# Sparse attention beside an RWKV recurrence: scores and weighted sums per head of 64 channels instead of in the 128-channel latent space

## The chip, the cores and the metric

The kernel runs on one core of one Trainium2 chip. The metric is the device time of one execution in microseconds (us), lower is better. The core's engines are named as in the profile: PE is TensorE, with PEld for its weight loads, DVE is VectorE, ACT is ScalarE, POOL is GpSimd, and SP is SyncE, which here only issues DMAs.

## The reference, cut to what is computed

One layer on a sequence of 2048 tokens of width 1024. A projection of the normalised input feeds two branches of 512 channels each, and an output projection adds their result to the input. The first branch is an RWKV recurrence in 8 heads of 64 channels. The second is attention in 8 heads of 64 channels, in which each query uses at most 256 keys, chosen by separate index heads; keys and values of all heads come from one latent vector of 128 channels per token.

```python
y_rwkv = rwkv7_branch(p_shift, g_rwkv, ...)
c_q, c_kv = rmsnorm(q_down, q_norm_g), rmsnorm(kv_down, kv_norm_g)      # 256 and 128 channels
q = (c_q @ w_uq).reshape(B, T, ATTN_HEADS, HEAD_DIM)
q_abs = jnp.einsum('bthd,hrd->bthr', q, w_uk) * (HEAD_DIM ** -0.5)      # query in the latent space
...
_, idx = lax.top_k(score, topk)                                         # the chosen keys
c_sel = jax.vmap(lambda c, i: c[i])(c_kv, idx)
s = jnp.einsum('bqhr,bqkr->bhqk', qa, c_sel)
p = jax.nn.softmax(s, axis=-1)
o_lat = jnp.einsum('bhqk,bqkr->bqhr', p, c_sel)
...
o = jnp.einsum('bthr,hrd->bthd', o_lat, w_uv)
y = jnp.concatenate([y_rwkv, o * silu(gate)], axis=-1) @ w_out
out = rmsnorm(x + y, final_g)
```

## The kernel before

The program has four parts, which a scheduler interleaves when the kernel is built; the order of the instructions on each engine is fixed from then on, and an engine whose next instruction waits does nothing else meanwhile.

**SA** (`phase_as`) projects the input, for four groups of 512 tokens, in blocks of 128 columns. Its matmuls are in fp32r, a single-pass form of lower precision, so each operand is split into a high and a low part and a product takes three passes (`proj`, L574 to L576). `visit` runs rounds of such blocks with small jobs between them; the index heads and the choice of keys (`picker`) write one mask per block of 128 queries. `latent` (L702) normalises the latent vector c_kv and stores it twice, channels first (`d_ckT`) and tokens first (`d_ck`), each as a high and a low part; the normalised query vector goes to `d_cq`.

**T** (`phase_t`) is the attention. An item is 256 queries of a pair of heads. `onto` brings the queries into the latent space (12 matmuls of 256 columns, L1171 to L1173). For each block of 128 queries and each head, scores come in chunks of up to 512 keys, in three passes (L1197 to L1199); DVE adds the mask and takes the maximum (L1201), ACT exponentiates each chunk (L1208). The weights are transposed on PE (L1217), copied by ACT as a high part (L1220), and DVE makes the low part (L1221). The weighted sums run for both heads together as 256 columns in three passes (L1225, L1226, L1229). At the end of an item the row sums are spread (L1238, L1241), and six matmuls of 256 columns lead out of the latent space (L1248 to L1250). The masks are loaded once, since the items go through the four pairs of heads for the same queries.

**R** (`phase_r`) is the recurrence, in 16 chunks of 128 tokens that depend on each other. `prepare(n)` loads and scales a chunk and makes its systems E (`prep`, L910, L912; issued with low priority through `later`); `inverse` inverts their 32x32 diagonal blocks on POOL: DMAs write E to DRAM (`du`, L950) and bring it back with a system on each partition (`A`, L952), 31 pairs of POOL instructions follow (L961, L963), and DMAs carry the result back (`dx` L964, `TT` L968). `prep2` makes what else the chain needs (L920 to L940). `chain` then takes the state through the two halves of the chunk: products with the state (L981, L988), `solve` (L997) with the inverses, L1015, `solve` again, the new state (L1022). `tail` normalises the result (L1032 to L1044; the power on POOL is in the helper `rpow`, L127) and writes it to `d_y` for two units in turn through one buffer `yo` (L1050 to L1054). In the program text `prepare(n + 1)` stands ahead of `chain(n)`.

**W** (`phase_w`) is the output projection: for each of 16 blocks of 128 tokens it loads `yl` from `d_y` (L1296), splits it, and runs 48 matmuls of 512 columns (L1306 to L1309); the result is added to the input, normalised and stored (L1310 to L1316). Its tiles lie where those of T lay, so W begins after T's end.

T and R share PE and the other engines. All DMAs of R and W and most of T's go through the one queue of SP in a fixed order; T's latents and queries go through POOL's.

Of the kernel before, what the change touches and what calls it, by code (L numbers as in the profile page):

```python
# [36 lines left out]
def kernel(ctx: ExitStack, tc: tile.TileContext, x, norm_g, w_in, mu_shift, w0, w_up, a0, a_up,  # L37
# [19 lines left out]
    # ------------------------------------------------------------------ scratch in DRAM  # L57
# [5 lines left out]
    d_ckT = [dram([128, T], F32, f"d_ckT{i}") for i in range(2)]  # L63
    d_ck = [dram([128, NB, 128], F32, f"d_ck{i}") for i in range(2)]
# [9 lines left out]
    # ------------------------------------------------------------------ constants  # L74
# [4 lines left out]
    ones2 = const([128, 2], F32, "ones2")          # columns: ones on rows 0-63, ones on rows 64-127  # L79
# [3 lines left out]
    bad = const([128, NB], F32, "bad")             # rows whose choice of keys is to be made again  # L83
# [49 lines left out]
    def later(n=1):  # L133
        """what is issued inside gives way to what is issued outside, and inside with less"""
# [50 lines left out]
def picker(e, tls, KI, wi_a, wi_s, fast, spare=None):  # L185
    """choice of keys"""
    tc, dma, V, S, G, PE, f32, nm = e.tc, e.dma, e.V, e.S, e.G, e.PE, e.f32, e.nm
    wqh = tls([128, 2, 4, 2, 64], F32R, "wqh")   # query projection of the index heads, each head twice
    wql = tls([128, 2, 4, 2, 64], F32R, "wql")
    cmask = tls([128, 128], F32, "cmask")        # -LOW where key <= query, else LOW  # L190

    def setup_s():
# [10 lines left out]
        # blocks 0 and 1 keep every key that is not after the query  # L203
# [7 lines left out]
    def queries(j):  # L211
        """q_idx^T of blocks 2j, 2j+1: [128 (twice the 64 channels), head, 256]; high and low parts"""
# [55 lines left out]
    def quick(b, xs, on_act):  # L268
        """the same from the scores in float16: bisection in the cube root of the threshold, then the exact
        threshold among the (at most eight) scores left; marks the rows where more than those were left"""  # L270
# [15 lines left out]
        # each column of vm holds a score, so at least 256 scores reach their minimum  # L286
# [15 lines left out]
        # cube roots of the ends (negated for the scalar engine's counts), and the halves of their distance  # L302
# [22 lines left out]
        # the eight largest of the rest, and the one wanted  # L325
# [9 lines left out]
        G.tensor_tensor(col(48), col(28), col(31), op=OP.subtract)       # how many of the equal scores stay  # L335
# [10 lines left out]
    def exact(b, xs, on_act):  # L346
        """largest threshold that at least TOPK scores reach, found bit by bit in an order-preserving
        integer form of the scores; then the additive mask, ties going to the lowest index"""
# [18 lines left out]
        def search(data, cnt0, cand, thr, res):  # L367
            """16 steps of bisection; cnt0: first of 16 columns for the counts; thr: TOPK or a column"""
# [17 lines left out]
        def rejected(cnt0, thr, res):  # L386
            """the largest count below the threshold"""
# [6 lines left out]
        # columns: 0-15, 16-31 counts; 32, 33 candidates; 34 top, 35 low; 36 counted above; 37 k2; 38 its form  # L394
# [53 lines left out]
def again(env):  # L448
    """the choice of keys by the general search, the attention and the output once more"""
# [23 lines left out]
def phase_as(env):  # L473
    """projections in, and the choice of keys"""
# [33 lines left out]
    # lora weights [decay | a]: high parts on rows 0-63, low parts on rows 64-127;  # L508
    # of each, rows 0-31 take the decay's inputs and rows 32-63 those of a
# [11 lines left out]
    def load_w(cols, pad=False, raw=None):  # L521
        """columns of w_in as high and low parts [128, 8, 128]; cols: (target, source, width)"""
# [56 lines left out]
    def shift(pm, blk, mu, om):  # L579
        """token shift of the psum block"""  # L580
# [37 lines left out]

    def split_store(t, dst, sl):
        """fp32 tile -> high and low parts -> dram"""  # L620
        h = t2(F32R)
        l = t2(F32R)
        S.activation(h, t, AF.Copy)
        V.tensor_tensor(l, t, f32(h), op=OP.subtract)
        dma(dst[0][sl], f32(h))
        dma(dst[1][sl], f32(l))

# [10 lines left out]
    def index_group(g, t, qr):  # L638
        """index keys and weights, and the queries' latent"""
# [34 lines left out]
        pb = row_spread(rsq, 1)  # L674
# [403 lines left out]
def phase_t(env):  # L1078
# [52 lines left out]
    for u in (uvh, uvl):  # L1131
        V.memset(f32(u)[:, :, 1], 0.0)
# [212 lines left out]
```

## Time and profile before

| | |
|---|---|
| median of 3 runs | 2168.61 us (2166.92 to 2169.61) |
| span of the profiled execution | 2172.8 us; its time is not listed apart from the span |
| PE busy | 1926.4 us, 89% of the span, 13094 instructions |
| DVE, ACT, POOL busy | 1457.3, 1095.8, 872.3 us |
| SA alone on PE | 0 to 895 us |
| T and R on PE | 895 to 1955 us; T's last instruction falls in chunk 15 of R's 16 |
| rest of R, and W | 1955 to 2172.8 us |

The span is that of one profiled execution, the times are those of runs of their own; the span is 4.2 us above their median. The page's busy times are sums over the whole span, so they are read by stage; the matmuls overlap in the pipeline, so the cost of one is taken from the distance of two starts rather than from its duration. In the chain of waits, a piece is followed back from the last instruction to what released it.

### The profile page before, as it was taken

The page shows a single profiled execution, that of the slowest core. Times are in us where ns is not written, and L with a number is a line of the kernel's source. Part 1 is how long each engine was busy: PE and PEld are TensorE (multiplying, and loading weights), DVE is VectorE, ACT ScalarE, POOL GpSimd, SP SyncE. Part 2 cuts the span into 40 slices and gives each one's busy share as a digit, 9 for nine tenths or more (in the row PEclk, how much of TensorE's full clock was granted, in tenths as well). Part 3 has the DMA queues.
Part 4 walks back from the last instruction along what each step waited for, and adds up shares of the span by engine and source line. Part 5 has one row for each costly group of instructions (what it writes and reads, how often), then busy time and mean ns, then how long its engine had stood idle before and what let it go on. Part 6 is the DMA issues. An engine that isn't in the chain of part 4 may idle for free. (4 is left out here: it accounts for less than half of the span.)

```text
span 2172.8 us, 37051 instructions
## 1 busy us (share of the span) xinstructions
PE 1926.4 (89%) x13094; PEld 1606.2 (74%) x13094; DVE 1457.3 (67%) x3331; ACT 1095.8 (50%) x2328; POOL 872.3 (40%) x2114
## 2 busy tenths in 40 slices
PE   5999988979788889788989889898898998887997
PEld 4787776757676677577878778787787887776886
DVE  5554597896969798676767766677566776554332
ACT  4345845345375444345555656565555565454221
POOL 1112325444344656445543454345444345442110
PEclk9899998989999999789999999999899999998999
DMA  7442432226243222633332223212222112116343
GB/s 240 154 128 59 128 128 68 92 68 241 65 142 118 74 73 68 197 80 81 80 80 52 58 61 92 58 39 76 62 59 73 53 33 63 47 33 201 122 148 108
DMA packets 255891, 206.69 MB, mean 95 GB/s; under 512 B 75088, under 2 KB 219856, under 8 KB 254544
## 3 DMA queue, kind: packets, MB, share of 16 engines
q1 hardware_dynamic: 244656, 183.78, 28.6%
q0 software_dynamic: 11040, 20.45, 3.2%
q8 instruction: 105, 1.72, 0.3%
q14 instruction: 90, 0.74, 0.1%
HBM read 127.31 MB, written 76.87 MB: 94 GB/s over the span
## 5 line engine op out<-in xcount | busy, mean ns | idle before, releaser
L574 PE MATMUL pm<-xh,wh 128*128 128x512 f32 x800 | 330.2, 415 | 20.7 <-DVE t L585 12.7
L575 PE MATMUL pm<-xl,wh 128*128 128x512 f32 x800 | 327.6, 410 | 0.0
L576 PE MATMUL pm<-xh,wl 128*128 128x512 f32 x800 | 326.6, 409 | 0.0
L1208 ACT ACTIVATE sc<-sc,mx 128x512 f32<-128x512 f32 (+3 forms) x320 | 206.9, 650 | 68.9 <-DVE mx L1206 68.4
L1201 DVE CUSTOM_DVE_ANT_0 sc<-s,mk 128x512 f32<-128x512 f32 (+3 forms) x320 | 188.5, 605 | 60.3 <-PE tr L1217 33.5
L1221 DVE TENSOR_TENSOR ptl<-tr,pth 128x512 fp32r<-128x512 f32 (+1 forms) x288 | 186.0, 654 | 52.0 <-ACT pth L1220 48.7
L1220 ACT ACTIVATE pth<-tr 128x512 fp32r<-128x512 f32 (+1 forms) x288 | 160.9, 570 | 116.6 <-PE tr L1217 95.2
L961 POOL TENSOR_TENSOR Xtmp<-Xr,A 128x60 f32<-128x60 f32 (+24 forms) x496 | 148.6, 300 | 165.6 <-DMA A<-du 131.5
L574 PEld LDWEIGHTS pm<-xh,wh 128*128 128x128 f32 x800 | 158.4, 199 | 61.6 <-DVE t L585 15.9
L1217 PE MATMUL tr<-ident,sc 128*128 128x128 f32 x1088 | 177.8, 282 | 18.0 <-DVE ptl L1221 12.6
L576 PEld LDWEIGHTS pm<-xh,wl 128*128 128x128 f32 x800 | 157.2, 196 | 35.8
L575 PEld LDWEIGHTS pm<-xl,wh 128*128 128x128 f32 x800 | 157.7, 197 | 35.1
L963 POOL TENSOR_TENSOR Xr<-Xr,Xtmp 128x60 f32<-128x60 f32 (+24 forms) x496 | 150.2, 303 | 34.6
L1225 PE MATMUL om<-pth,ck 128*128 128x256 f32 x544 | 159.0, 312 | 0.8 <-DVE ga L1251 0.8
L1197 PE MATMUL s<-ckT,qh 128*128 128x512 f32 (+2 forms) x320 | 135.7, 424 | 26.7 <-DVE mx L1201 26.1
L1217 PEld LDWEIGHTS tr<-ident,sc 128*128 128x128 f32 x1088 | 131.4, 145 | 25.2 <-DVE ptl L1221 13.0
L314 ACT ACTIVATE mk<-x,st 128x1920 bf16<-128x1920 f16 (+5 forms) x72 | 98.0, 1361 | 100.1 <-POOL st L311 100.1
L1226 PE MATMUL om<-pth,ck 128*128 128x256 f32 x544 | 146.5, 289 | 0.0
L246 ACT ACTIVATE rl<-lg,wi 128x512 f32<-128x512 f32 (+3 forms) x152 | 93.0, 628 | 94.3 <-DVE xs L251 41.0
L1229 PE MATMUL om<-ptl,ck 128*128 128x256 f32 x544 | 127.7, 311 | 14.4 <-DVE ptl L1221 14.4
L317 DVE TENSOR_SCALAR_CACHE_REDUCE mk<-x,st 128x2048 bf16<-128x2048 f16 (+5 forms) x72 | 120.7, 1676 | 1.5
L1199 PE MATMUL s<-ckT,ql 128*128 128x512 f32 (+2 forms) x320 | 118.4, 380 | 3.4 <-DVE ql L1175 3.4
(345 smaller groups left out, 4790.7 us busy)
## 6 DMA issues: line engine op xcount, KB each, us to landing
wraw<-in_w_in_dram SPq DMA_DIRECT2D x42, 512.0 KB
d_rw<-t SPq DMA_DIRECT2D x80, 256.0 KB
ld<-d_rw SPq DMA_DIRECT2D x32, 640.0 KB
A<-du SPq DMA_DIRECT2D x16, 512.0 KB
yl<-d_y SPq DMA_DIRECT2D x16, 512.0 KB
xr<-in_x_dram SPq DMA_DIRECT2D x16, 512.0 KB
out_dram<-xr SPq DMA_DIRECT2D x16, 512.0 KB
cq<-d_cq POOLq DMA_DIRECT2D x30, 256.0 KB, 3.8
```

The costliest lines, as they stand in the source:

```text
L574: PE.matmul(pm, wh[:, k], XH[g][:, k], start=k == 0, stop=False)
L575: PE.matmul(pm, wh[:, k], XL[g][:, k], start=False, stop=False)
L576: PE.matmul(pm, wl[:, k], XH[g][:, k], start=False, stop=k == KD - 1)
L961: G.tensor_tensor(tmp[:, :m, :w], Xr[:, :m, s:s + 1].to_broadcast([128, m, w]), A[:, s:s + 1, s + 1:].to_broadcast([128, m, w]), op=OP.mult)
L963: G.tensor_tensor(Xr[:, :m, s + 1:], Xr[:, :m, s + 1:], tmp[:, :m, :w], op=OP.add)
L1201: V.tensor_tensor_reduce(out=sc[:, :w], in0=pS[:, :w], in1=mks[qb][:, c0:c0 + w], scale=1.0, scalar=LOW, op0=OP.add, op1=OP.max, accum_out ...
L1208: S.activation(sc[:, :w], sc[:, :w], AF.Exp, bias=mx[:, 4:5], accum_out=sums4[:, q, h, i:i + 1])
L1217: PE.transpose(pt[:, i, h], PR[h][(kb + i) // 4][0][:, (kb + i) % 4 * 128:(kb + i) % 4 * 128 + 128], ident)
L1220: S.activation(th[:, :m], pt[:, :m], AF.Copy)
L1221: V.tensor_tensor(tw[:, :m], pt[:, :m], f32(th)[:, :m], op=OP.subtract)
L1225: PE.matmul(pof, ck[0][:, kb + i], rh, start=kb + i == 0, stop=False)
L1226: PE.matmul(pof, ck[1][:, kb + i], rh, start=False, stop=False)
```

## The change

The attention works per head. SA now projects onto the heads: `query_weights` and a query job of 96 matmuls of 512 columns make q for 64 channels per head (`d_q`, high and low parts); behind `latent`, `keys_of` and `values_of` (48 matmuls of 512 columns each) make keys (`d_kt`, high and low) and values (`d_vt`, tokens first) of the heads, which replaces 16 transposes and the storing of `d_ckT` and `d_ck`. In T a unit is 128 queries of a pair of heads, and the units go through all 16 blocks for one pair and then for the next, so each mask is loaded four times. The 128 rows of a key tile hold the 64 channels of a head as a high part and below it as a low part, and the query tile holds its high (or low) part twice; two passes then give the scores. One exponential runs over the whole row of a head. The transposed weights stay in fp32, without a low part, and the weighted sums are fp32 matmuls of 128 columns onto 64 output rows, one head in each half of the array. All of T's loads are now on SP's queue: 64 masks, 256 query pieces, 64 key pieces, 16 value tiles, 64 gates, and 64 stores. Per execution T has 2944 PE instructions, and had 4380. R and W are unchanged, with line numbers 60 and 4 higher.

```diff
+        def keys_of(p):
+            def job():
+                h, l = parts
+                pk = pst([128, 512], "tr", 2)
+                ws = slice(p * 128, p * 128 + 128)
+                PE.matmul(pk, wh[:, 0, ws], h, start=True, stop=False)
+                PE.matmul(pk, wh[:, 0, ws], l, start=False, stop=False)
+                PE.matmul(pk, wl[:, 0, ws], h, start=False, stop=True)
+                split_store(pk, e.d_kt, (slice(None), p, slice(g * 512, g * 512 + 512)))
+            return job
...
+        rows = [tl([128, T], F32, "sc", 4) for h in range(2)]
...
+            for h in range(2):
+                pS = pst([128, C], "s", 2)
+                PE.matmul(pS[:, :wp], qh[:, h, qs], k[:, h, :wp], start=True, stop=False)
+                PE.matmul(pS[:, :wp], ql[:, h, qs], k[:, h, :wp], start=False, stop=True)
...
+            S.activation(rows[h][:, :n], rows[h][:, :n], AF.Exp, bias=mx[:, h, 4:5], accum_out=sums[:, h:h + 1])
...
-                    PE.matmul(pof, ck[0][:, kb + i], rh, start=kb + i == 0, stop=False)
-                    PE.matmul(pof, ck[1][:, kb + i], rh, start=False, stop=False)
...
-                    PE.matmul(pof, ck[0][:, kb + i], rl, start=False, stop=kb + i == qb)
...
+        def values(kb, m, w):
+            for i in range(m):
+                v = VT[p, (kb + i) // 4]
+                for h in range(2):
+                    PE.matmul(po[HALF[h]], v[:, (kb + i) % 4, HALF[h]], w[:, i, h],
+                              start=kb + i == 0, stop=kb + i == b)
...
+    units = [(p, b) for p in range(NP) for b in range(NB)]
```

In the order rows below, a row is one instruction or a run of equal ones: line, operation, output and inputs, shape, and how many. First PE inside T, before: `tr` are the transposes, `s` the scores, `om` the weighted sums.

```order
L1229 MATMUL om_20461<-ptl_20483,ck_2111_13334 128x256 x2
L1225 MATMUL om_20461<-pth_20497,ck_2111_13334 128x256
L1226 MATMUL om_20461<-pth_20497,ck_2112_13335 128x256
L1225 MATMUL om_20461<-pth_20497,ck_2111_13334 128x256
L1226 MATMUL om_20461<-pth_20497,ck_2112_13335 128x256
L1217 MATMUL tr_20507<-ident,sc_20410 128x128
L1217 MATMUL tr_20507<-ident,sc_20441 128x128
L1217 MATMUL tr_20507<-ident,sc_20410 128x128
L1217 MATMUL tr_20507<-ident,sc_20441 128x128
L1197 MATMUL s_20664<-ckT_2109_13332,qh_20197 128x512
L1198 MATMUL s_20664<-ckT_2110_13333,qh_20197 128x512
L1199 MATMUL s_20664<-ckT_2109_13332,ql_20198 128x512
```

And PE inside T with the change:

```order
L1237 MATMUL tr_19196<-ident,sc_19041 128x128
L1237 MATMUL tr_19196<-ident,sc_19042 128x128
L1237 MATMUL tr_19196<-ident,sc_19041 128x128
L1237 MATMUL tr_19196<-ident,sc_19042 128x128
L1237 MATMUL tr_19203<-ident,sc_19041 128x128
L1237 MATMUL tr_19203<-ident,sc_19042 128x128
L1237 MATMUL tr_19203<-ident,sc_19041 128x128
L1237 MATMUL tr_19203<-ident,sc_19042 128x128
L1203 MATMUL s_19192<-kt_19088,q_3596_19031 128x256
L1204 MATMUL s_19192<-kt_19088,q_3597_19036 128x256
L1246 MATMUL om_19173<-pt_19179,vt_18452 64x128 x4
L1246 MATMUL om_19173<-pt_19186,vt_18452 64x128 x3
```

The three passes of 256 columns over `pth` and `ptl` have become runs of mostly four fp32 matmuls of 128 columns on 64 output rows, alternately in the two halves of the array; T has 273 such runs, and they stand between transposes and scores, which use the whole array.

Second, PE in a late chunk of R, from the middle of `chain`: before, with T's work (`s`, `om`, `tr`) beside it.

```order
L1015 MATMUL ch_11921<-SV_11437,E_11298 32x64
L1015 MATMUL ch_11921<-SV_11457,E_11334 32x64
L1197 MATMUL s_20645<-ckT_2109_13332,qh_20197 128x384
L1198 MATMUL s_20645<-ckT_2110_13333,qh_20197 128x384
L1199 MATMUL s_20645<-ckT_2109_13332,ql_20198 128x384
L1229 MATMUL om_20461<-ptl_20468,ck_2111_13334 128x256 x2
L1217 MATMUL tr_20492<-ident,sc_20410 128x128
L1217 MATMUL tr_20492<-ident,sc_20441 128x128
L1217 MATMUL tr_20492<-ident,sc_20410 128x128
L1217 MATMUL tr_20492<-ident,sc_20441 128x128
```

The same place with the change, in a chunk after T's end, where `po` is W's:

```order
L1075 MATMUL ch_12281<-SV_11890,E_11767 32x64
L990 MATMUL rp_12267<-ident,BK_12132 128x128 x4
L1057 MATMUL ch_12281<-R_12280,TT_11860 32x64 x8
L1310 MATMUL po_20848<-wh_20136,yh_20840 128x512
L1311 MATMUL po_20848<-wl_20137,yh_20840 128x512
L1310 MATMUL po_20848<-wh_20136,yh_20840 128x512
L1311 MATMUL po_20848<-wl_20137,yh_20840 128x512
L1310 MATMUL po_20848<-wh_20136,yh_20840 128x512
L1311 MATMUL po_20848<-wl_20137,yh_20840 128x512
L1310 MATMUL po_20848<-wh_20136,yh_20840 128x512
```

T's last instruction now falls at the end of R's chunk 8; in chunks 9 to 16 only W stands beside the chain. Ahead of the second solve of chunks 9 to 16 stand 242, 432, 480, 528, 576, 624, 672 and 720 of W's 768 matmuls, so from chunk 11 on one block of 48 falls in each chunk, in four pieces inside the chain: behind the first half's second solve, behind its new state, and on both sides of the second half's reads. It is the block whose `yl` comes from the chunk just ended.

Third, SP's queue around the loads of the inverse: before.

```order
L950 DMA du_10975<-E_10924 32x8x32 x2
L950 DMA du_10975<-E_10960 32x8x32 x2
L1054 DMA d_y<-yo_10886 128x2x128
L952 DMA A_10977<-du_10975 128x1x1024
L1048 DMA gr_10895<-d_gr 128x2x128
L874 DMA ld_11313<-d_rw 128x10x128
L878 DMA vt_11278<-d_v 128x2x192
L1054 DMA d_y<-yo_10894 128x2x128
L1048 DMA gr_11261<-d_gr 128x2x128
```

With the change, in a late chunk:

```order
L1010 DMA du_12156<-E_12105 32x8x32 x2
L1114 DMA d_y<-yo_12067 128x2x128
L1010 DMA du_12156<-E_12141 32x8x32 x2
L1108 DMA gr_12076<-d_gr 128x2x128
L934 DMA ld_12494<-d_rw 128x10x128
L1012 DMA A_12158<-du_12156 128x1x1024
L1114 DMA d_y<-yo_12075 128x2x128
L1108 DMA gr_12442<-d_gr 128x2x128
L938 DMA vt_12459<-d_v 128x2x192
L1300 DMA yl_20841<-d_y 128x8x128
```

The `A` of chunk n + 2 stood behind the two `du` and the first `d_y<-yo` of chunk n, and now a 640 KB `ld` stands ahead of it too; the second `d_y<-yo` stays behind `A`, and W's `yl` for chunk n is now behind that store at once.

## Rows read from the trace of the kernel before

**Rows 1.** Busy time by stage: start:end, length, PE, PEld, DVE, ACT, POOL, PEclk, DMA share, GB/s

```profile
0.00:895.00 895.00, 776.08 (x3448) 620.23 (x3448) 670.51 (x1235) 437.68 (x678) 352.56 (x684) 0.93 0.36 115
895.00:1955.00 1060.00, 955.52 (x8528) 827.80 (x8529) 705.03 (x1998) 596.39 (x1528) 488.39 (x1349) 0.93 0.27 68
1955.00:2172.80 217.80, 194.80 (x1120) 158.13 (x1119) 81.77 (x99) 61.77 (x123) 31.34 (x83) 0.95 0.45 145
```

**Rows 2.** Groups of instructions: count, then busy us and mean ns, then idle before

```profile
L1225 PE MATMUL om<-pth,ck 128*128 128x256 f32 x544 | 159.0, 312 | 0.8 <-DVE ga L1251 0.8
...
L1199 PE MATMUL s<-ckT,ql 128*128 128x512 f32 (+2 forms) x320 | 118.4, 380 | 3.4 <-DVE ql L1175 3.4
...
L1171 PE MATMUL om<-cq,wch 128*128 128x256 f32 x128 | 38.5, 303 | 0.7 <-DVE mx L1206 0.7
```

**Rows 3.** PE's timeline in W: start us, duration, instruction

```profile
2073.53 0.39 PE L1306 MATMUL po<-wh,yh 128*128 128x512 f32 x1
...
2077.15 1.98 PE L1309 MATMUL po<-wh,yl 128*128 128x512 f32 x8
```

**Rows 4.** PE's timeline in a chain: an x8 here is 4 fp32 matmuls

```profile
1424.03 0.66 PE L981 MATMUL ch<-S,X 128*64 128x128 f32 x8
1424.52 0.63 PE L988 MATMUL ch<-SV,E 128*64 128x64 f32 x16
```

**Rows 5.** The chain of waits, T and R on PE: start us, length, piece

```profile
1289.50 0.59 PE rp L981 x8
...
1290.55 0.32 PE om L1229
1290.87 0.12 PE om L1225
...
1293.29 0.44 PE rp L981 x8
...
1297.23 0.44 PE tr L1217 x4
```

**Rows 6.** SP's timeline: issues of A; first two and last of 16

```profile
941.93 0.83 SPq L952 DMA_DIRECT2D A<-du  x1
...
985.97 0.56 SPq L952 DMA_DIRECT2D A<-du  x1
...
1930.31 0.56 SPq L952 DMA_DIRECT2D A<-du  x1
```

**Rows 7.** POOL's timeline: first and last step of the last chunk's inverse

```profile
1940.26 0.24 POOL L961 TENSOR_TENSOR Xtmp<-Xr,A 128x31 f32<-128x31 f32 x1 [10.19 <-DMA A<-du]
...
1963.58 0.22 POOL L963 TENSOR_TENSOR Xr<-Xr,Xtmp 128x8 f32<-128x8 f32 x1
```

**Rows 8.** The chain of waits: a store issued right behind A

```profile
1930.98 9.49 DMA d_y<-yo
```

**Rows 9.** ACT's timeline at R's end: idle before and releaser in brackets

```profile
2046.32 0.39 ACT L1026 ACTIVATE y<-rp 128x256 f32<-128x256 f32 x1
...
2063.74 0.81 ACT L1050 ACTIVATE yo<-ch,gnb,gng 128x128 f32<-128x128 f32 x2 [3.60 <-DMA d_y<-yo]
...
2077.61 1.06 ACT L1297 ACTIVATE yh<-yl 128x1024 fp32r<-128x1024 f32 x1 [2.44 <-DMA yl<-d_y]
```

**Rows 10.** DVE's timeline, the same stretch

```profile
2052.11 0.68 DVE L1041 TENSOR_TENSOR y<-y,gst 128x512 f32<-128x512 f32 x1
```

**Rows 11.** SP's timeline, the same stretch

```profile
2061.80 0.37 SPq L1054 DMA_DIRECT2D d_y<-yo  x1
...
2073.72 0.52 SPq L1296 DMA_DIRECT2D yl<-d_y  x1
```

**Rows 12.** Two windows of 10 us at T's beginning, columns as in rows 1

```profile
950.00:960.00 10.00, 5.06 (x45) 4.24 (x42) 3.15 (x14) 2.42 (x7) 5.10 (x18) 0.79 0.34 95
960.00:970.00 10.00, 9.27 (x40) 8.29 (x39) 6.50 (x19) 3.96 (x11) 7.12 (x21) 0.52 0.08 20
```

**Rows 13.** The chain of waits behind the last matmul

```profile
2160.77 0.70 DVE xr L1310
```

More of the change, by code (lines that the diff above doesn't have):

```diff
@@ L674, in index_group @@
         pb = row_spread(rsq, 1)
+        ch = tls([128, 2, 512], F32R, "qh")
+        cl = tls([128, 2, 512], F32R, "ql")
         for j in range(2):
             V.scalar_tensor_tensor(qr[j], qr[j], e.qgc[:, j:j + 1], pb, op0=OP.mult, op1=OP.mult)
-            split_store(qr[j], e.d_cq, (slice(None), j, slice(g * 512, g * 512 + 512)))
+            split(qr[j], ch[:, j], cl[:, j])
+        dma(e.d_cq[0][:, :, sl], f32(ch))
+        dma(e.d_cq[1][:, :, sl], f32(cl))
+        for p in range(NP):
+            pq = pst([128, 512], "pm", 3)
+            cs = slice(p * 128, p * 128 + 128)
+            for j in range(2):
+                PE.matmul(pq, uq[0][:, j, cs], ch[:, j], start=j == 0, stop=False)
+                PE.matmul(pq, uq[0][:, j, cs], cl[:, j], start=False, stop=False)
+                PE.matmul(pq, uq[1][:, j, cs], ch[:, j], start=False, stop=j == 1)
+            split_store(pq, e.d_q, (slice(None), p, sl))
     def lora(pm, g):
@@ L802, in phase_as @@
     ws = index_weights()
+    query_weights()
     x_group(3)
@@ new lines, in queries_in, with scores @@
+    def queries_in(p, c):
+        Q[p, c] = []
+        for i in range(2):
+            q = tl([128, 2, 256], F32R, f"q{i}", 2)
+            for h in range(2):
+                for s in range(2):
+                    dma(f32(q)[HALF[s], h], e.d_q[i][HALF[h], p, c * 256:c * 256 + 256])
+            Q[p, c].append(q)
+    def scores(p, b, out):
+        n = (b + 1) * 128
+        mk = tl([128, T], BF16, "mk", 3)
+        dma(mk[:, :n], e.d_mask[b])
+        if b % 2 == 0:
+            queries_in(p, b // 2)
+        qs = slice(b % 2 * 128, b % 2 * 128 + 128)
+        qh, ql = Q[p, b // 2]
+        rows = [tl([128, T], F32, "sc", 4) for h in range(2)]
+        mx = tl([128, 2, 8], F32, "mx", 3)
+        sums = tl([128, 2], F32, "sums", 3)
+        for nt, c0 in enumerate(range(0, n, C)):
+            w = min(C, n - c0)
+            wp = max(w, 256)
+            if (p, nt) not in KT:
+                chunk_in(p, nt)
+            k = KT[p, nt]
+            for h in range(2):
+                pS = pst([128, C], "s", 2)
+                PE.matmul(pS[:, :wp], qh[:, h, qs], k[:, h, :wp], start=True, stop=False)
+                PE.matmul(pS[:, :wp], ql[:, h, qs], k[:, h, :wp], start=False, stop=True)
+                V.tensor_tensor_reduce(out=rows[h][:, c0:c0 + w], in0=pS[:, :w], in1=mk[:, c0:c0 + w],
+                                       scale=1.0, scalar=LOW, op0=OP.add, op1=OP.max,
+                                       accum_out=mx[:, h, nt:nt + 1])
+            yield
+        nt = (n + C - 1) // C
+        for h in range(2):
+            V.tensor_reduce(mx[:, h, 4:5], mx[:, h, :nt], axis=AX.X, op=OP.max, negate=True)
+            S.activation(rows[h][:, :n], rows[h][:, :n], AF.Exp, bias=mx[:, h, 4:5], accum_out=sums[:, h:h + 1])
+        out.extend((rows, sums))
@@ new lines, in attend, with weights @@
+    def attend(p, b, rows, sums):
+        ts = slice(b * 128, b * 128 + 128)
+        rs = tl([128, 2, 2], F32R, "rs", 2)
+        V.reciprocal(sums, sums)
+        S.activation(rs[:, 0], sums, AF.Copy)
+        V.tensor_tensor(rs[:, 1], sums, f32(rs)[:, 0], op=OP.subtract)
+        pf = pst([128, 2, 128], "om", 2)
+        PE.transpose(pf[0:4, 1], f32(rs).rearrange("p a b -> p (a b)"), ident)
+        rh = tl([4, 128], F32R, "rh", 2)
+        S.activation(rh, pf[0:4, 1], AF.Copy)
+        PE.matmul(pf[:, 0], sel, rh, start=True, stop=True)
+        ga = tl([128, 128], F32, "ga", 3)
+        dma(ga, e.d_ga[p][:, ts])
+        V.tensor_tensor(ga, ga, pf[:, 0], op=OP.mult)
+        yield
+        po = pst([128, 128], "om", 2)
+        def weights(kb, m):
+            pt = pst([128, 2, 2, 128], "tr", 2)
+            for i in range(m):
+                for h in range(2):
+                    PE.transpose(pt[:, i, h], rows[h][:, (kb + i) * 128:(kb + i) * 128 + 128], ident)
+            w = tl([128, 2, 2, 128], F32, "pt", 4)
+            S.activation(w[:, :m], pt[:, :m], AF.Copy)
+            return w
+        def values(kb, m, w):
+            for i in range(m):
+                v = VT[p, (kb + i) // 4]
+                for h in range(2):
+                    PE.matmul(po[HALF[h]], v[:, (kb + i) % 4, HALF[h]], w[:, i, h],
+                              start=kb + i == 0, stop=kb + i == b)
+        left = []
+        for kb in range(0, b + 1, 4):
+            now = [(k, min(2, b + 1 - k)) for k in range(kb, min(kb + 4, b + 1), 2)]
+            now = [(k, m, weights(k, m)) for k, m in now]
+            for x in left:
+                values(*x)
+            left = now
+            yield
+        for x in left:
+            values(*x)
+        V.tensor_tensor(ga, ga, po, op=OP.mult)
+        dma(e.d_y[:, 4 + p, ts], ga)
@@ L1270, in phase_w @@
+    units = [(p, b) for p in range(NP) for b in range(NB)]
+    last = None
+    for u in units + [None]:
+        out = []
+        parts = [scores(*u, out)] if u else []
+        if last:
+            parts.append(attend(*last))
+        while parts:
+            parts = [g for g in parts if next(g, parts) is not parts]
+        last = (*u, *out) if u else None
 def phase_w(env):
```

228 lines of the change are left out of this document (55 added, 173 removed).

## The prediction

> **What bounds the kernel now.** I read first the table of busy time by stage [rows 1]: SA holds PE for 895 us, T with R for 1060 us, and the last 217.8 us are the end of R and W. In the middle stage PE is busy 955.5 of 1060 us while no other engine is above 705, so there PE's stream sets the time. Next I read prices from PE's timelines and the chain of waits. Sixteen W matmuls of 512 columns take 3.62 us from the start of the first to that of the seventeenth [rows 3], 0.227 each; one of 256 columns takes 0.12, a transpose 0.11 [rows 5]. An fp32 matmul of 128 columns into 64 rows, the halves alternating as in the chain of R, takes 0.49 / 4 = 0.122 [rows 4]. A change between such half-width work and whole-array work costs about 0.15 on the way in (0.59 against 0.44 for the same eight records) and 0.20 on the way out (0.32 against 0.12) [rows 5].
>
> Then R by itself. A is issued 44 us after the one before it at the very beginning, where little stands in the way, and then every 67 us (1930.31 less 985.97, over 14 intervals) [rows 6]: today R follows PE's stream and is not driven by its own loop. That is why I count T by its parts and R by what is left.
>
> T by its parts: three score passes of 320 instructions, of on average 448 columns, 3 x 64 = 191 us; three weighted-sum passes of 544 of 256 columns, 196 [rows 2]; 1088 transposes 120; 384 matmuls onto the latent (three lines of 128 [rows 2]) 46; 192 out of it 23; row sums 12. Together 588. The stage holds nearly all of the first 15 chunks of R, say 14.75: (1060 - 588) / 14.75 = 32 us per chunk, its own matmuls, its changes of array width and the waits it brings.
>
> **The change part by part.** SA gains 96 + 48 + 48 = 192 matmuls of 512 columns, 43.6 us, less 16 transposes, and about 8 for its jobs' waits: between 40 (they fill idle PE: SA has 119 us of it [rows 1]) and 60; I take 50, so SA ends at 945.
>
> T loses one score pass, -64. The weighted sums lose 196 and gain 1088 x 0.122 = 133, and 273 changes in and out of half width. Their price is bounded below by nothing (the array keeps streaming) and above by the 0.35 of [rows 5]; I take 0.30, 82 us, near the upper end, because those rows show exactly such a change. The sums come out at +19, so what looked like the big saving is none. Queries onto the latent go, -46, the way out -23, the spreading of sums per 128 queries +6, T's preparation of weights -8 (16 + 16 small products and the waits between them, an estimate). Together -116: T = 472. DVE's low parts, L1221, and 60% of the exponentials' instructions go too; I cost them at nothing, because PE covers them. PE idles 104 us in that stage [rows 1], 7 per chunk; if that work was the cause, T's stage would end 8 x 7 = 56 us earlier, my lower end there.
>
> The changing of array width is where the Trainium skill speaks against this change: "TensorEngine Tiling (Array Packing)", section "Key Properties", says that a change of tiling mode drains TensorE. The rows agree, with 0.15 and 0.20 us. By a mode change without cost T would be 390.
>
> Where T ends. The order puts R's chunk 8 at T's last instruction, instead of chunk 15. So the stage is 472 + 8 x 32 = 728, and T ends at 945 + 728 = 1673, 282 us earlier than now. But then eight chunks of R are left, with only W beside them, where today one and a half are left.
>
> **What a late chunk takes.** Let e be the end of a chunk's chain, the copy of y [rows 9], 2046.3. The tail's normalised y is there 6.5 us later [rows 10]; a transpose, the first yo on ACT and two POOL steps make it e + 9.5, and in a quiet queue the first store lands 1.9 us after its issue [rows 9, 11] and frees yo. The second yo is ready at e + 14.5. Meanwhile DVE, which has the tail's work ahead of the masks of E for chunk n + 2, lets du go out, and A is issued at about e + 13, behind ld. A takes 10 us even with no load ahead of it (1940.26 less 1930.31) [rows 6, 7], and the second store, behind it, does too [rows 8]: it lands at about e + 25. W's yl then takes 4 us [rows 9, 11]: e + 30. Only then can PE pass the W block that stands inside chain n + 1: yh 1 us, 48 x 0.227 = 11, and what remains of that chain, three dependent steps on PE and ACT of nearly 2 us each, the new state, three reads and the copy, together 12 to 13. The next e is 55 us after this one.
>
> The bounds: below, POOL's loop, since the inverse alone is 23.5 us [rows 7], its wait for A 10, and what POOL does for tail and preparation about 11: 44, the first spacing of [rows 6]. Above, 67, the spacing of today. I take 55, for it follows the order step by step.
>
> The sum: 1673, then chunk 9, which has 242 W matmuls (55 us) and some 20 of its own, 75; chunk 10 with 190 of them (43) and 25, 68; six chunks of 55, 330; then the last tail without an inverse, e + 21 for yl, one W block 11 and the 12 us behind the last matmul [rows 13], 45. Together **2191**, against a span of 2172.8. The median of the runs is 4.2 below that span, so **2187** against 2168.6: slower by 0.8%. The time taken out of T comes back as R's chunks running alone. (A measurement here tells about 0.2% from no change.)
>
> **Rivals.**
> *POOL's loop sets the late chunks.* If the stores do not queue behind A, yl comes at about e + 20 and the period falls to 44: 6 x 11 = 66 less, 2121, faster. For it: the 44 of [rows 6], the 1.9 us store. Against: the second store stands behind A in SP's order. The point where faster begins is a period of 52.
> *Width changes cost nothing* because loads of weights hide them: 82 less, 2105. For it: PEld idles 22% of T's stage [rows 1]. Against: [rows 5].
> *The clock.* In a window in which PE was busy 5.1 of 10 us the granted clock was 0.79, and in the next, with 9.3 busy, 0.52 [rows 12]: after half-idle stretches PE runs at the lower level, 1.2 GHz. Late chunks have PE busy about 30 of 55 us (11 for W, some 20 for the chunk), with a long wait ahead of each W block. If every block runs at the lower level, 11 more per chunk for W alone: 6 x 11 = 66, or 2253. Against: today's last stage stands at 0.95 [rows 1], but it is full. "TensorE: Matmul & The Clock Gate" of the Trainium skill, section "HAM oscillation — how this bites in real kernels", describes that case, a kernel whose bursts alternate with waits on DMA and start slow each time.
> *T's loads block R on SP.* Some 530 DMAs of T now stand in the queue with A, du and TT, each in its order and many waiting for a tile to be free. One A of 10 us in front of a load that PE waits for, per chunk, is 80: 2267. Against: key and query tiles are loaded one unit ahead and more.
> *The halves do not overlap* in T: each matmul then costs the two halves after one another, about 0.1 more, 110: 2297. Against: it is the form of [rows 4], alternating in the same way.
>
> **How the numbers follow.** The forecast itself 0.33; POOL's loop 0.30; free width changes 0.10; the clock 0.12; SP 0.10; halves 0.05. The forecast's own range, T's stage 56 shorter or 20 longer and a period of 52 to 60, is about 2115 to 2235. For the range: 2100 takes in POOL's loop, which rests on rows, and most of the free changes; 2275 the clock and SP; outside stay the halves and combinations of two. Faster: the two faster rivals, 0.40, and a fifth of the forecast's 0.33, where its range lies below 2164, less 0.05 for cases in which a faster rival meets a slower one: 0.42. Within 0.2%: 0.06, from the forecast's range. Slower: the rest, 0.52.
>
> **What would show it.** SA ends at about 945 on PE. T's groups: scores in two lines of 320, weighted sums 1088 of a pitch near 0.122 with the first matmul behind a run at 0.3. T's last matmul at about 1673, with R's eighth inverse behind it. From there, issues of A 55 us apart, and in the chain of waits A, the store behind it and yl in turn, with PE idle some 20 us per chunk. If A's issues are 44 apart, POOL's loop was the bound; if the granted clock of those windows is near 0.6, the clock; if T's last matmul is later than 1720, SP or the halves, which the pitch of the weighted sums tells apart. A period under 52, or T's end before 1650, makes the sign wrong.

## The result, and the profile after

The changed kernel takes 2256.91 us (median of 4 runs, 2249.86 to 2260.81), the kernel before 2169.11 beside it: a ratio of 1.0403, with a 95% interval of 1.0379 to 1.0428. It is slower by 4.0%, where 0.8% was forecast; the sign and the range held, the size did not. The profiled execution has a span of 2256.6 us and a time of 2258.54, so its span can be set against the 2191 of the sum.

Busy time by stage after the change, with the columns of [rows 1]; the cuts are T's first and last matmul and the end of the chunk behind it:

```profile
0.00:980.00 980.00, 834.44 (x3624) 663.91 (x3624) 699.63 (x1281) 455.64 (x710) 359.20 (x700) 0.91 0.38 124
980.00:1695.00 715.00, 663.64 (x6118) 489.85 (x6118) 390.82 (x1345) 421.80 (x893) 245.58 (x690) 0.94 0.43 119
1695.00:1812.00 117.00, 104.85 (x770) 82.55 (x770) 57.99 (x89) 42.08 (x85) 65.35 (x162) 0.89 0.50 156
1812.00:2256.60 444.60, 298.27 (x2398) 232.03 (x2396) 151.27 (x272) 106.46 (x247) 201.31 (x531) 0.72 0.26 75
```

SA is 85 us longer (895 before). T is 345 us shorter and still bound by PE, which idles 51 of 715 us. Behind T there are 562 us instead of 217.8, and in the last 445 of them PE is busy for two thirds, at a granted clock of 0.72. So T gave back what was asked of it, and more than that went to the two ends.

The groups of matmuls that answer to [rows 2]:

```profile
L1246 PE MATMUL om<-pt,vt 128*64 128x128 f32 x2176 | 191.3, 290 | 0.2
...
L1203 PE MATMUL s<-kt,q 128*128 128x512 f32 (+2 forms) x320 | 148.9, 466 | 33.4 <-DVE mx L1205 18.2
L1204 PE MATMUL s<-kt,q 128*128 128x512 f32 (+2 forms) x320 | 124.1, 389 | 9.9 <-DMA q<-d_q 9.9
```

There are two passes of scores, and 2176 records of weighted sums (two to a matmul, so 1088). Their price is read from the distance of starts, in PE's timeline of T:

```profile
1120.74 0.66 PE L1246 MATMUL om<-pt,vt 128*64 128x128 f32 x8
1121.33 0.66 PE L1237 MATMUL tr<-ident,sc 128*128 128x128 f32 x4
1121.92 0.65 PE L1246 MATMUL om<-pt,vt 128*64 128x128 f32 x6
...
1502.72 1.09 PE L1246 MATMUL om<-pt,vt 128*64 128x128 f32 x16
1503.74 1.16 PE L970 MATMUL rp<-X,BK 64*128 64x128 f32 x8
```

Eight matmuls take 1.02 us and four 0.59: about 0.11 for one. From one run of weighted sums to the next, with four transposes between, 1.18 us pass; four matmuls and four transposes at 0.11 are 0.88 of that, so a run costs 0.30, in and out together. The forecast had 0.122 and 0.30.

Where SA and T begin and end on PE: the first matmul of the index heads, then T's first and last matmul:

```profile
208.16 0.39 PE L245 MATMUL lg<-KI,qh 128*128 128x512 f32 x1
...
980.46 0.55 PE L1203 MATMUL s<-kt,q 128*128 128x256 f32 x1 [11.04 <-DMA kt<-d_kt]
...
1694.36 0.69 PE L1246 MATMUL om<-pt,vt 128*64 128x128 f32 x2
```

SP's queue: the last mask that SA stores, and the first and three late issues of A, which answer to [rows 6]:

```profile
965.43 0.32 SPq L346 DMA_DIRECT2D d_mask<-mk  x1
...
1080.42 0.66 SPq L1012 DMA_DIRECT2D A<-du  x1
...
1900.06 0.67 SPq L1012 DMA_DIRECT2D A<-du  x1
...
1955.71 0.68 SPq L1012 DMA_DIRECT2D A<-du  x1
...
2010.93 0.68 SPq L1012 DMA_DIRECT2D A<-du  x1
```

The late issues are 55.7 and 55.2 us apart. The first one is a surprise: it comes 100 us behind T's first matmul, where before 47 lay between the stage's start at 895 [rows 1] and the first A [rows 6].

The chain of waits through one late chunk, from the normalising of one chunk to that of the next (start, length, piece):

```profile
1941.98 0.70 DVE gst L1092
...
1957.25 0.73 POOL yo L1113
1957.99 8.60 DMA d_y<-yo
1966.61 4.25 DMA yl<-d_y
1970.88 1.06 ACT yh L1301
1971.99 0.80 PE po L1310
...
1989.42 0.59 PE ch L1057 x16
...
1994.27 1.11 PE ch L1082 x16
...
1997.19 0.70 DVE gst L1092
```

This is the chain of the forecast, piece by piece: the second yo, its store beside A (8.60 us where a quiet one takes 1.9), yl, the block of W that stands inside the next chunk's chain, the rest of that chain. It repeats after 55.2 us.

### The profile page after: what moved, and what is told of

Same layout as the page of the kernel before. It is cut to its first block, busy times and chain, and to the rows that moved or that the text cites. A ratio compares the mean times of both kernels' runs of the same rounds, so it can differ in the third digit from the quotient of the medians.

```text
span 2256.6 us, 36571 instructions
## 1 busy us (share of the span) xinstructions
PE 1901.2 (84%) x12906; PEld 1468.3 (65%) x12906; DVE 1299.7 (58%) x2986; ACT 1026.0 (45%) x1934; POOL 871.4 (39%) x2082
## 4 chain that ended last, share of the span: by engine, by line
PE 25%; DMA 11%; POOL 7%; issue 4%; DVE 2%; ACT 1%; SPq 1%; POOLq 0%; ACTq 0%; DVEq 0%
PE om L1246 5%; PE tr L1237 4%; DMA d_y<-yo 3%; PE s L1203 3%; DMA A<-du 2%; PE s L1204 2%; POOL Xr L1023 2%; POOL Xtmp L1021 2%; PE rp L970 2%; PE po L1310 1%; PE po L1311 1%; PE po L1313 1%; DMA yl<-d_y 1%; DMA dx<-Xr 1%; DMA ld<-d_rw 1%
## 5 line engine op out<-in xcount | busy, mean ns | idle before, releaser
L1239 ACT ACTIVATE pt<-tr 128x512 f32<-128x512 f32 (+1 forms) x288 | 159.2, 569 | 119.9 <-PE tr L1237 118.8
L1246 PE MATMUL om<-pt,vt 128*64 128x128 f32 x2176 | 191.3, 290 | 0.2
L1237 PE MATMUL tr<-ident,sc 128*128 128x128 f32 x1088 | 186.1, 288 | 0.2 <-ACT sc L1212 0.2
L1212 ACT ACTIVATE sc<-sc,mx 128x128 f32<-128x128 f32 (+15 forms) x128 | 153.1, 1197 | 65.1 <-DVE mx L1211 64.4
L1203 PE MATMUL s<-kt,q 128*128 128x512 f32 (+2 forms) x320 | 148.9, 466 | 33.4 <-DVE mx L1205 18.2
L1023 POOL TENSOR_TENSOR Xr<-Xr,Xtmp 128x60 f32<-128x60 f32 (+24 forms) x496 | 157.4, 317 | 36.3
L1246 PEld LDWEIGHTS om<-pt,vt 128*64 128x64 f32 x2176 | 124.5, 139 | 51.9 <-issue 39.2
L1310 PE MATMUL po<-wh,yh 128*128 128x512 f32 x256 | 111.6, 438 | 53.8 <-ACT yh L1301 53.8
L1204 PE MATMUL s<-kt,q 128*128 128x512 f32 (+2 forms) x320 | 124.1, 389 | 9.9 <-DMA q<-d_q 9.9
L970 PE MATMUL rp<-X,BK 64*128 64x128 f32 x512 | 93.4, 332 | 23.4 <-DVE E L972 14.7
```

What stands on the lines that cost most here:

```text
L1023: G.tensor_tensor(Xr[:, :m, s + 1:], Xr[:, :m, s + 1:], tmp[:, :m, :w], op=OP.add)
L1203: PE.matmul(pS[:, :wp], qh[:, h, qs], k[:, h, :wp], start=True, stop=False)
L1204: PE.matmul(pS[:, :wp], ql[:, h, qs], k[:, h, :wp], start=False, stop=True)
L1212: S.activation(rows[h][:, :n], rows[h][:, :n], AF.Exp, bias=mx[:, h, 4:5], accum_out=sums[:, h:h + 1])
L1237: PE.transpose(pt[:, i, h], rows[h][:, (kb + i) * 128:(kb + i) * 128 + 128], ident)
L1239: S.activation(w[:, :m], pt[:, :m], AF.Copy)
```

## The experiments

**What made SA longer: the queries.** Two kernels leave out one of the two new sets of products. Without queries:

```diff
-            pq = pst([128, 512], "pm", 3)
...
-                PE.matmul(pq, uq[0][:, j, cs], ch[:, j], start=j == 0, stop=False)
...
-            split_store(pq, e.d_q, (slice(None), p, sl))
+            dma(e.d_q[0][:, p, sl], f32(ch)[:, p % 2])
+            dma(e.d_q[1][:, p, sl], f32(cl)[:, p % 2])
```

> Leaves out the 96 query products of SA and their evictions (the stores of d_q stay, with other data; the output is not the layer's). Theory: the products cost more than their 22 us because they stand ahead of the choice of keys, which then starts and ends later, and because PE runs at the lower clock around them; SA's last projection matmul comes back from 964.6 us to about 910. Rival: only their matmuls count, and it comes to about 942.

Without keys and values (the same for `split_store(pk, e.d_kt, ...)` and for the copies of `pv`):

```diff
-                split_store(pk, e.d_kt, (slice(None), p, slice(g * 512, g * 512 + 512)))
+                dma(e.d_kt[0][:, p, g * 512:g * 512 + 512], f32(h))
+                dma(e.d_kt[1][:, p, g * 512:g * 512 + 512], f32(l))
```

> Leaves out the 96 products that make keys and values per head, and their evictions (the stores stay, with other data). Theory: these stand among the projections, beside the choice of keys, so they cost about their matmuls, 22 to 30 us: SA's last projection matmul at 935 to 943. Rival: DVE sets SA's pace and each of its added evictions costs; then about 923, as much as half of the 82 us that SA gained.

Without queries the last projection lies at 887.0, earlier than the 910 that was expected, T begins at 946 and the kernel takes 2196.06 us (one run), 61 less; the products themselves are worth 22. Without keys and values the last projection lies at 931.8, 33 earlier where 22 to 30 were expected, and yet T begins at 982, where it did: 2244.29 (one run), 13 less. In these kernels T's start does not follow SA's last projection. It follows the choice of keys: the last mask is stored at 965 without keys and values, at 928 without queries, at 965.43 with both. From the first matmul of the index heads to that store 757 us pass (965.43 - 208.16), before the change 747:

```profile
140.42 0.40 PE L243 MATMUL lg<-KI,qh 128*128 128x512 f32 x1
...
887.29 0.32 SPq L344 DMA_DIRECT2D d_mask<-mk  x1
```

(PE's and SP's timeline of the kernel before.) So the choice of keys is a chain of some 750 us whose start sets its end, and that start is 68 us later. Part of this shows in the clock. The stretch from 40 to 200 us, columns as in rows 1, first after, then before:

```profile
40.00:200.00 160.00, 130.89 (x588) 105.06 (x586) 66.63 (x139) 51.06 (x96) 16.45 (x20) 0.81 0.45 158
```

```profile
40.00:200.00 160.00, 153.94 (x750) 125.80 (x749) 82.53 (x161) 68.87 (x118) 25.67 (x42) 0.94 0.41 136
```

PE has more to do after the change and does less of it: 131 us busy instead of 154, at a granted clock of 0.81, while the new weights are loaded and prepared. Without queries the index heads begin at 171, not at 140, so the products account for 37 of the 68. That kernel keeps the preparing of the weights and the stores; q_mid below, which moves these too, begins at 166. What makes the 25 us that are left there was not taken apart. That x_noq gains 61 where T starts 35 earlier fits its trace: its first A goes out at 924.5, before T begins, and at T's end 8.6 chunks of R are done, one more than with the queries (7.6).

**R ahead of T.** T ends with R in chunk 8. If the place of R's preparation in the order makes that, a higher priority for it moves chunks back under T:

```diff
-        with e.later():
+        with e.later(0):
```

(twice, in `prepare` and around the tail.)

> The changed kernel with the recurrence's preparation and tail no longer given way to attention; its order has R at chunk 10 to 11 of 16 when T ends instead of chunk 8. Theory: the loss lies in R's chunks that run without T beside them, 57 us each where one beside T costs 32; two and a half chunks fewer there give 2.5 x 25 = 62, and the 19 us that chunk 9 lost behind the inverse: 2175 to 2200. Rival: the waits of R's loop only move into T's stage, and the time stays above 2235.

The kernel takes 2204.54, ratio 1.0166 [1.0132, 1.0200], so 52 us of the 88 lost come back. The first A goes out 14 us behind T's first matmul, not 100. T's stage grows from 714 to 806 us and holds 10.7 chunks where it held 7.6: 30 us for each one more. That is the price of a chunk beside T which the forecast had as 32. A chunk alone takes 55 or more, and this difference is what comes back here. The same edit in the kernel before is the control:

> The kernel before with the same edit to R's priority, nothing else. Theory: there R is at chunk 14 when T ends, as without the edit (15), since T's stage is long enough for R, so the edit moves it by less than 20 us either way: 2150 to 2190. Rival: R first is better for any kernel of this shape, and this one goes below 2140.

There it gains nothing, it costs 12 us: 2180.02, ratio 1.0055 [1.0035, 1.0075]. With R in chunk 15 at T's end, no chunks are left to bring back.

**Which wait sets 55 us.** The forecast says the second store behind A, the rival POOL's loop. A on ACT's queue takes it out of the store's way in SP's order:

```diff
-        dma(A.rearrange("l s t -> l (s t)"),
+        S.dma_start(A.rearrange("l s t -> l (s t)"),
```

> The changed kernel with the load A of the inverse issued by ACT instead of SP. Theory: in a late chunk the second store of the tail and then W's load wait behind A in SP's queue, so without A there the chunk falls from 55 us to about 46 and six of them give 50: about 2205. Rival: the transfers share the 16 DMA engines whatever queue they come from, or POOL's loop holds the chunk; then within 10 us of 2257.

2256.96, ratio 1.0395 [1.0370, 1.0420]: nothing. The second store, issued at 1958.78 on SP, now stands behind no A in its own queue, and still yl follows it only at 1967.18, 8.4 us later:

```profile
1953.79 1.86 DMA d_y<-yo
...
1956.55 10.83 DMA A<-du
1967.44 0.25 POOL Xtmp L1021
...
1992.07 0.22 POOL Xr L1023
```

(The chain of waits of this kernel.) The first store, with nothing beside it, took 1.86. So the store's wait is still there, and A's place in its queue is not what makes it. Store and A end together, at 1967.2 and 1967.4, so it is likely that they share DMA engines; but the 640 KB `ld` stands ahead of the store in SP's queue in both kernels and was not moved. The end of A's transfer, columns as in rows 1:

```profile
1964.00:1967.00 3.00, 1.27 (x18) 0.82 (x16) 0.00 (x0) 0.00 (x0) 0.00 (x0) 0.50 0.26 94
```

A mean share of 0.26 is, as an estimate, the work of about four of the 16 DMA engines: A's 10 us may be long because it uses few of them. Spreading it over more was not tried.

The rows show a second thing. The chain now runs through POOL: A 10.8 us, the inverse 24.9, then 19 of W's statistics, the new state, tail, yo, du and issue until the next A, which makes 55 again. So two loops of about 55 us run here side by side, through the store and through POOL. Since the store's wait was not taken away, this run does not tell which of them holds the period.

A second buffer for yo tests the other side of the store, the wait of the tail for its buffer:

```diff
-            yo = tl([128, 2, W], F32, "yo", 1)
+            yo = tl([128, 2, W], F32, "yo", 2)
```

> The changed kernel with two buffers for yo instead of one, so that the tail's second half doesn't wait for the first store, and the next chain not for it either; its order has R at chunk 10 when T ends instead of chunk 8. Theory: two chunks fewer run alone (2 x 25 = 50), and a late chunk loses the 3 us that yo waited for its store and its first read: 2190 to 2210. Rival: the loops through A, its store and W's load set the late chunk in any case and T's stage only grows: above 2235.

2196.39, ratio 1.0140 [1.0123, 1.0158]: 60 us better. But the late chunks still end 54 to 57 us apart for three of the last four (1934, 1989, 2046, 2101, 2144). The gain lies beside T instead, which ends in chunk 10, at 1747. One buffer held R back where T covers it. In late chunks the period stays, and what holds it there was not separated.

**Does half-width work cost what the forecast said?** Here the weighted sums go through the whole array, 544 fp32 matmuls of 256 columns, half of whose output is not used (the product with the gate is then made per head):

```diff
-        po = pst([128, 128], "om", 2)
+        po = pst([128, 2, 128], "om", 2)
...
-                for h in range(2):
-                    PE.matmul(po[HALF[h]], v[:, (kb + i) % 4, HALF[h]], w[:, i, h],
-                              start=kb + i == 0, stop=kb + i == b)
+                PE.matmul(po.rearrange("p a b -> p (a b)"), v[:, (kb + i) % 4], w[:, i].rearrange("p a b -> p (a b)"),
+                          start=kb + i == 0, stop=kb + i == b)
```

> The changed kernel with the weighted sums as 544 whole-array fp32 matmuls of 256 columns for both heads, half of whose result is not used, so that no change of array width stands in T. Theory as in the prediction: 1088 x 0.122 and 273 changes at 0.30 are 215 us, the whole-array form 544 x 0.43 is 234, so T is 19 us longer. Rival from the changed kernel's own trace: 0.108 per matmul and 0.2 per run are 172 us, T is 62 longer; by costless changes it would be over 100 longer. T's stage holds more chunks of R by this order, so its length is compared at 32 us per chunk.

2284.72 us (one run). T's stage is 822 us with 9.4 chunks; less 32 each that is 521, against 714 less 7.6 x 32 = 471. The difference of 50 is far from the 114 of changes that cost nothing (544 x 0.43 = 234 for the whole array, less 1088 x 0.11 = 120). It lies above the 19 of the forecast's prices and the 32 that 0.11 and 0.30 give; the rival's 0.2 for a run leaves out part of what the rows above show. So a change of width costs. This one run would put it at 0.23 for the pair, the rows at 0.30, and the 18 us between them are not explained.

**Queries at another time.** If the query job delays the choice of keys, it belongs behind the start of that. First beside the projections of the round "r2 gr2", with the normalised queries read back through POOL's queue into the buffers `xt`:

```diff
+            c.append(tl([128, D], F32R, "xt", 2).rearrange("p (a b) -> p a b", a=2))
+            G.dma_start(c[i], e.d_cq[i][:, :, sl])
...
+                hq = heads_queries(g) if names == "r2 gr2" else None
...
+                    if hq:
+                        hq(2 * wi_)
+                        hq(2 * wi_ + 1)
```

> The changed kernel with the query products moved from the index heads, ahead of the choice of keys, to the round of projections r2 gr2, beside the choice; all work is done. Theory: their place costs, not their matmuls. Leaving them out gave 61 us, 22 us of which are the matmuls; moved, about 35 come back, T's first matmul goes from 980 us to about 950, and the time to about 2220. Rival: DVE sets the pace of SA wherever the products stand, T's first matmul stays above 970 and the time above 2245.

> Both edits: the query products moved beside the choice of keys, and R's preparation and tail no longer given way to T. Theory: the two losses are apart (one ends with SA, the other lies behind T's end), so they add: 2204 less 35 is about 2170, level with the kernel before (2150 to 2185). Rival: R's chunks take up what SA gives back, and the time stays at 2195 or more.

The second adds R's priority. They take 2286.02 (1.0526 [1.0497, 1.0555]) and 2225.89 (1.0263 [1.0240, 1.0286]). The first half of the theory held: the index heads begin at 169 and the last mask is stored at 925, 40 earlier. But the last projection now lies at 1010 and T begins at 1022, in part because PE waits for loads into buffers that the choice of keys still held. PE's waits from 800 to 1010 us:

```profile
PE tr L710 <- DMA xt<-d_cq: 15.8, 1, 15.8
PE tr L711 <- DMA xt<-d_cq: 10.7, 1, 10.7
```

That is 26.5 us on PE, of the 45 by which the last projection is later (the 59 named below is too much).

A round of its own between "r2 gr2" and "k2 v2", loaded by SP into the buffers of the weights, avoids that:

```diff
-    mix(visit((0, 1), ["r0 gr0 k0", "lora v0 ga0", "kv r1", "gr1 k1", "v1 ga1", "r2 gr2", "k2 v2", "ga2 r3", "gr3 k3",
+    mix(visit((0, 1), ["r0 gr0 k0", "lora v0 ga0", "kv r1", "gr1 k1", "v1 ga1", "r2 gr2", "q", "k2 v2", "ga2 r3", "gr3 k3",
...
+            c.append(tl([128, KD, 128], F32R, ("wh", "wl")[i], 3).rearrange("p a b -> p (a b)").rearrange("p (a b) -> p a b", a=2))
+            dma(f32(c[i]), e.d_cq[i][:, :, sl])
```

> The query products between the projection rounds r2 gr2 and k2 v2, in the buffers of the projection weights and loaded by SP, so that they wait for nothing of the choice of keys; all work is done. In the run before, PE waited 59 us for their loads, behind buffers that the choice of keys held. Theory: the choice of keys is a chain of about 755 us and its start sets its end; with the products away from its start the first index-head matmul is back at 140 to 170 us, the last mask at 895 to 930, T's first matmul at 930 to 955, and the time at 2205 to 2230. Rival: the projections then end last, T's first matmul stays at 970 or later and the time at 2245 or more.

> The same with R's preparation and tail no longer given way to T. Theory: SA's loss and the loss behind T's end are apart, so 30 to 50 come off the 2204 of R first alone: 2155 to 2175, level with the kernel before or below it. Rival: 2195 or more.

2227.27, ratio 1.0280 [1.0259, 1.0301]: 30 us less than the change, for a start of T that is 26 earlier. Index heads, last mask, T's first matmul, and the stretch from 40 to 200 us in this kernel:

```profile
165.86 0.40 PE L245 MATMUL lg<-KI,qh 128*128 128x512 f32 x1
...
929.89 0.32 SPq L346 DMA_DIRECT2D d_mask<-mk  x1
...
954.79 0.55 PE L1218 MATMUL s<-kt,q 128*128 128x256 f32 x1 [11.01 <-DMA kt<-d_kt]
```

```profile
40.00:200.00 160.00, 152.73 (x749) 126.03 (x748) 73.67 (x149) 62.82 (x109) 22.98 (x31) 0.94 0.40 135
```

That stretch is as it was before the change, clock and all. Here the last projection, at 942.95, lies behind the last mask, and T's loads go out behind both in SP's queue; so it is SA's end that T waits for. With R's priority on top it takes 2168.62 (12 runs), ratio 1.0003 [0.9988, 1.0019]. The two edits give 30 and 52 apart and 88 together, which is all of the loss.

**The version that beats both.** To these two it adds the second yo and a third buffer for the query tiles:

```diff
-            q = tl([128, 2, 256], F32R, f"q{i}", 2)
+            q = tl([128, 2, 256], F32R, f"q{i}", 3)
```

> All edits together: query products between the projections, R's preparation and tail not given way to T, two buffers for yo, three for T's query tiles. Its order has R at chunk 12 when T ends. Theory: on top of 2168.6 without the two buffers, one and a half chunks fewer alone give some 35, and T's 27 us of waits for query tiles shrink: 2115 to 2145, faster than both kernels by 1 to 2.5%. Rival: T and R together are bound by PE (7 of 10 us of a chunk's 72 in T's stage are T's), so what leaves the end is added to T's stage: within 15 us of 2168.

2124.37 against 2166.55 beside it: ratio 0.9811 [0.9786, 0.9835], 1.9% faster than the kernel before. By stage, columns as in rows 1 (SA, T, the next two chunks, the rest):

```profile
0.00:965.00 965.00, 825.30 (x3640) 659.15 (x3640) 708.53 (x1303) 460.39 (x715) 358.24 (x708) 0.93 0.41 134
965.00:1791.00 826.00, 752.82 (x7419) 567.98 (x7420) 454.46 (x1495) 471.30 (x1024) 381.39 (x1073) 0.92 0.43 116
1791.00:1958.00 167.00, 148.92 (x984) 115.38 (x980) 79.71 (x121) 53.19 (x108) 79.94 (x196) 0.90 0.50 149
1958.00:2127.50 169.50, 123.66 (x872) 97.06 (x870) 47.48 (x71) 38.51 (x88) 45.70 (x105) 0.84 0.27 80
```

T still begins 70 us later than before and ends 164 us earlier, with 12 chunks done, and 336 us are left behind it instead of 562. What the third query buffer alone is worth was not tried, nor a second yo in the kernel before.

## Why the prediction was right and wrong

The span is 65.6 us above the sum of 2191, and 61 of that lie in four lines, T's first matmul to chunk 9. The terms, as measured against as forecast:

| step | forecast | measured | off by |
|---|---|---|---|
| T's first matmul | 945 | 980.5 | +35 |
| T's stage | 728 | 713.9 | -14 |
| chunk 8 behind T's end | 0 | 21.3 | +21 |
| chunk 9 | 75 | 94.4 | +19 |
| chunk 10 | 68 | 68.8 | +1 |
| six late chunks | 330 | 331.6 | +2 |
| the end | 45 | 46.1 | +1 |

**Right: the mechanism.** T's gain came back as chunks of R running alone, and a late chunk takes 55 us by the pieces that were forecast: six of them took 331.6. The reason given for one piece did not hold: the store waits some 8 us without an A ahead of it in its queue too (a_act). And POOL's loop closes at the same 55. That the term came out to 2 us is in part luck. Two rows show where the first chunk behind T ends and where the last does, on ACT's timeline (copies of y of chunks 8 and 16):

```profile
1715.67 0.38 ACT L1086 ACTIVATE y<-rp 128x256 f32<-128x256 f32 x1
...
2210.51 0.38 ACT L1086 ACTIVATE y<-rp 128x256 f32<-128x256 f32 x1 [2.12 <-PE rp L1048]
```

**Wrong: "SA gains 50".** It gained 85. The step priced the new matmuls and their waits as so much work on PE, bounded by 40 and 60. It did not ask what was queued behind them. The query job stands ahead of the index heads, which start the choice of keys, and that chain of 750 us, not PE's work, decides when T can begin. x_nokv shows that T waits for the masks, q_mid that moving the queries gives 26 of the 35 us back.

**Wrong: "the order puts R's chunk 8 at T's last instruction".** T's last matmul fell in the midst of chunk 8, of which 21 us were left. A place in the order was read as an end.

**Wrong: chunk 9 at 75.** It was priced by PE's work, but its inverse was still running on POOL when T ended. The chain of waits there:

```profile
1725.16 1.10 POOL Xtmp L1021
...
1728.41 4.68 DMA dx<-Xr
...
1734.18 1.67 POOL gst L129
1735.87 1.53 DVE y L1101
```

POOL ends the inverse at 1728.4, waits for dx, and only then runs the tail's power at 1734.2, for which y waits. An inverse of about 39 us instead of the 23.5 of [rows 7], and a tail behind dx, are of the size of the 19 us.

**T's stage** came within 14 us, and r_first found 30 for the 32 of a chunk beside T. The 14 are about the part of chunk 8 that fell behind T's end: 714 less 7.6 x 32 is 471, where 472 was forecast. Inside, the price of a change of width held, and that of a matmul was a little high: by the rows the weighted sums cost 202 (1088 x 0.11 and 273 x 0.30), not 215. Some 12 us of other waits took that place. They were not separated; the idle time in front of the scores (33.4 and 9.9 us in their two lines) is more than that.

**The rivals.** POOL's loop was put at 44 and is 55 in the chain of a_act, since what stands between an inverse and the next A is 19 us and not the 11 assumed. Free changes of width are excluded by x_full. SP with T's loads did not decide: T's stage was not longer than forecast. The halves do overlap, at 0.11 for a matmul. The clock came in part. In one late chunk, columns as in rows 1:

```profile
1960.00:1971.00 11.00, 2.70 (x38) 1.75 (x37) 1.68 (x4) 1.33 (x5) 3.88 (x14) 0.62 0.50 155
1971.00:1977.00 6.00, 5.01 (x13) 3.99 (x14) 2.43 (x4) 2.29 (x4) 4.91 (x14) 0.57 0.16 47
1977.00:1990.00 13.00, 12.99 (x128) 9.96 (x126) 3.88 (x8) 2.50 (x6) 9.78 (x35) 1.00 0.06 17
```

After a stretch with PE busy for 2.7 of 11 us, W's block starts at a granted clock of 0.57: its first ten matmuls stand 0.43 apart (512 columns at the lower level, 1.2 GHz), the later ones 0.23. That is 2 us per block, where the rival had 11. "TensorE: Matmul & The Clock Gate" of the Trainium skill, section "HAM oscillation — how this bites in real kernels", describes such bursts that start slow; the trace agrees in kind and prices it at those 2 us.

## What to carry to other kernels

Work that is added to a phase is priced by what is queued behind it: if a long dependent chain starts there, its start sets the end, and a job of 22 us can cost 30 or more. When two interleaved phases share an engine and one gets shorter, what was balanced against it must be moved forward with it, or the saved time returns as the other phase running alone (here 30 us per chunk under cover, 55 without). When an edit is to remove a wait, look first whether it did, and work out the period of the other loop as well: here the store's wait stayed, and POOL's loop took 55 too.

## What was not expected of the hardware

A store of 128 KB takes 8.4 us beside A even from another queue, and 1.9 with no A beside it. And a step of POOL's inverse, 0.3 us as a rule, takes over 1 us while DVE works on two large operands. POOL's and DVE's timelines at the same moment:

```profile
1717.38 1.31 POOL L1023 TENSOR_TENSOR Xr<-Xr,Xtmp 128x54 f32<-128x54 f32 x1
```

```profile
1717.32 1.23 DVE L1302 TENSOR_TENSOR yl<-yl,yh 128x1024 fp32r<-128x1024 f32 x1
```

"SBUF — State Buffer" of the Trainium skill, section "SBUF: two separate sides", says that such a DVE operation and GpSimd lock each other out of shared ports. The trace agrees: 1.31 us beside 1.23. It was no term of the forecast. In chunk 9's inverse nine of the 62 steps took over 0.9 us, each beside a DVE operation of this size: some 8 of the 15 us by which it is longer.
